# Second layer's second MLP product as seven half-size products, with sums of its rows made in the loop of the first product

## The chip, the cores and the metric

The kernel runs on one core of one Trainium2 chip. The metric is the device time of one execution in microseconds (us), as the median of several runs. The profile is that of one execution; times in it are counted from its first instruction.

## The reference

A two-layer encoder works on 1024 tokens of width 1024. Each layer adds three blocks to the residual stream x, each as `x = x + rms_norm(block(rms_norm(x)))`: a mixer (pooling and short convolution in the first layer, a state-space scan and a long convolution in the second), a cross attention to 256 memory rows, and an MLP. Everything is fp32. What the change touches is the MLP of the second layer:

```python
def squared_relu_mlp(xn, w1, w2):      # w1: 1024 x 4096, w2: 4096 x 1024
    h = jax.nn.relu(xn @ w1)
    return (h * h) @ w2

h = rms_norm(x, norm_mlp[i, 0])
x = x + rms_norm(squared_relu_mlp(h, mlp_w1[i], mlp_w2[i]), norm_mlp[i, 1])
```

## The kernel before, in words

Activations lie transposed, features on the 128 partitions and tokens along the row, in two halves of 512 tokens (`hf`). Every fp32 operand is split into a high part (fp32r, copied by ScalarE, L252) and a low remainder (subtracted by VectorE, L255 through L234), and every product is three matmuls, high by high, high by low and low by high (`mm3`, L259 to L263). A weight block of 128 x 1024 comes through `wblk` (L265): a DMA on SP's queue into one of two `raw` buffers, then the split into one of four `wp` buffers.

**First MLP product** (`mlp_up`, L675). It is already one step of Strassen's scheme over output features and tokens. The loop "ue" (L708, eight turns) makes the part that needs only the first operands, stores partial sums in DRAM (`P1`) and the first quarter of the hidden rows in DRAM (`HID`). The loop "up" (L728, sixteen turns) makes five more products per turn, of four k-blocks each, that is 5 x 4 x 3 = 60 matmuls of 512 columns. VectorE makes four weight sums (L734 to L737), two splits, a third split of half the size, and five additions of 128 x 512 (L751 to L761). ScalarE applies relu and square (L702). POOL's queue loads `P1` and stores the finished hidden rows, three DMAs a turn.

**Second MLP product** (`mlp`, L766). The hidden rows are cut in eight blocks `c` of 512. For each block, four weight blocks `np_` (256 output features each) meet both token halves: `down1` (L782) runs 2 x 4 x 3 = 24 matmuls of 512 columns into one PSUM tile, and VectorE adds the tile to an accumulator in SBUF (L794). Hidden rows come back from DRAM on POOL's queue two blocks of 128 x 1024 at a time (`load`, L772) and are split again. That is 8 x 4 x 2 x 24 = 1536 matmuls, of which the last 96 (block 7, second half) run as 192 matmuls of 256 columns (`last`, L803), so that the norm and the output of the first 256 tokens lie beside the matmuls of the others. `residual` (L380) ends a half: sum of squares, a norm factor made by TensorE and VectorE (`rms`, L307), scaling, addition of x, and the store.

**What sets the order.** The program is written as one sequence of generators; a scheduler places each engine's instructions ahead of time by the order of the program and by free buffers. Work under `high_priority` is placed before other work that is ready. Within an engine, and within a DMA queue, the order is then fixed: an instruction that waits holds all that is behind it. Buffers: `hp` 9 tiles of 8 KB a partition, `act` 8 of 8 KB, `wp` 4, `raw` 2, `tp` 3, `np` 3, PSUM 3 tiles of two banks (`mmp`) and 2 of one (`aux`).

Before the second MLP stands the cross attention (`attention`, L627): scores and softmax, then the output product (`proj_out`, L418) with its two residuals, whose loads and stores go over POOL's queue (L394, L400).

## Time and profile before

| | us |
|---|---|
| median of 3 runs | 2927.45 (2925.89 to 2929.41) |
| the profiled execution, its own time | 2933.49 |
| its span, first to last instruction | 2931.7 |
| TensorE busy / VectorE busy / ScalarE busy | 2804.3 / 1968.8 / 1046.2 |
| second layer, loop "ue" | from 2242 to 2335.5 |
| second layer, loop "up" | from 2335.5 to 2564 |
| second layer, second MLP product | from 2564 to 2914.5 |
| norm and output after the last product | from 2914.5 to 2931.7 |

How to read it: the three medians differ by 3.5 us, 0.12%. A busy time counts the time in which an engine had an instruction in work; for TensorE the instructions overlap, so that the distance between starts tells its rate, not the length of one. The stages above are cut where the first matmul of each starts in the trace.

### The profile page before, as it was taken

To read this page: it belongs to the slowest core of one execution; us is meant where nothing else is said; L and a number is where in the kernel's file an instruction comes from. 1 tells how busy PE (TensorE), PEld (TensorE's weight loads), DVE (VectorE), ACT (ScalarE), POOL (GpSimd) and SP (SyncE) were. 2 spreads that over 40 slices of the span, in tenths; PEclk is the share of its full clock that TensorE was granted. 3 is DMA by queue.
4 is the path that set the end of the run, shared out by engine and by line. 5 is a ranking of instruction groups with operands and counts; after the bars stand their busy time and mean duration, and the time that the engine had idled before them with its cause. 6 is when DMAs were issued, how large, how long until landed. Compare 5 with 4: busy or idle time off the path is not lost. (4 is left out here: it accounts for less than half of the span.)

```text
span 2931.7 us, 35820 instructions
## 1 busy us (share of the span) xinstructions
PE 2804.3 (96%) x14024; PEld 2343.6 (80%) x14024; DVE 1968.8 (67%) x3287; ACT 1046.2 (36%) x1260; POOL 219.8 (7%) x403
## 2 busy tenths in 40 slices
PE   7998999999999999999999898899999999999997
PEld 7877888988777877888788787678988788788886
DVE  6676546838898756794877777946738866534446
ACT  4353324434544441222342311243434544422210
POOL 0000000001211110010100000000001211100000
PEclk9999999999999999999999999999999999999999
DMA  5582214224644454342447778734226644433313
GB/s 176 212 280 101 69 51 136 96 86 164 225 173 151 151 189 131 115 160 68 155 152 236 258 240 283 251 122 137 87 72 209 233 150 149 160 119 101 103 56 115
DMA packets 159057, 448.81 MB, mean 153 GB/s; under 512 B 16356, under 2 KB 61544, under 8 KB 151848
## 3 DMA queue, kind: packets, MB, share of 16 engines
q1 hardware_dynamic: 79736, 219.81, 23.4%
q0 software_dynamic: 48496, 200.30, 19.7%
q10 hardware_dynamic: 30656, 26.41, 2.7%
q8 instruction: 110, 1.80, 0.3%
q14 instruction: 59, 0.48, 0.1%
HBM read 330.07 MB, written 116.39 MB: 152 GB/s over the span
## 5 line engine op out<-in xcount | busy, mean ns | idle before, releaser
L263 PE MATMUL mdn<-hdn,wdn 128*128 128x512 f32 x640 | 250.1, 391 | 0.0
L261 PE MATMUL mdn<-hdn,wdn 128*128 128x512 f32 x640 | 249.7, 390 | 0.0
L262 PE MATMUL mdn<-hdn,wdn 128*128 128x512 f32 x640 | 249.7, 390 | 0.0
L234 DVE TENSOR_TENSOR aup<-aup,mdn 128x1024 f32<-128x1024 f32 x108 | 131.5, 1218 | 169.8 <-PE mdn L263 169.6
L261 PE MATMUL mup<-apre,wup 128*128 128x512 f32 x384 | 151.9, 395 | 8.1 <-DVE hup L234 8.1
L234 DVE TENSOR_TENSOR hup<-hup,mup 128x512 f32<-128x512 f32 x128 | 87.5, 684 | 98.1 <-PE mup L263 96.9
L262 PE MATMUL mup<-apre,wup 128*128 128x512 f32 x384 | 150.3, 391 | 0.0
L263 PE MATMUL mup<-apre,wup 128*128 128x512 f32 x384 | 150.2, 392 | 0.0
L262 PEld LDWEIGHTS mdn<-hdn,wdn 128*128 128x128 f32 x640 | 120.3, 188 | 25.3 <-issue 0.6
L261 PEld LDWEIGHTS mdn<-hdn,wdn 128*128 128x128 f32 x640 | 120.4, 188 | 24.9 <-issue 0.2
L263 PEld LDWEIGHTS mdn<-hdn,wdn 128*128 128x128 f32 x640 | 120.3, 188 | 24.9
L252 ACT ACTIVATE wdn<-rdn 128x1024 fp32r<-128x1024 f32 x54 | 57.1, 1057 | 223.1 <-PE mdn L263 210.2
L252 ACT ACTIVATE wup<-rup 128x1024 fp32r<-128x1024 f32 x66 | 69.4, 1060 | 180.6 <-PE mup L263 165.7
L261 PE MATMUL msc<-wsc,hpre 128*128 128x256 f32 x448 | 127.9, 286 | 1.6 <-ACT hpre L252 1.6
L262 PE MATMUL msc<-wsc,hpre 128*128 128x256 f32 x448 | 128.9, 288 | 0.0
L263 PE MATMUL msc<-wsc,hpre 128*128 128x256 f32 x448 | 128.1, 287 | 0.4 <-DVE hpre L234 0.4
L262 PE MATMUL mmx<-hpre,wmx 128*128 128x512 f32 x320 | 124.7, 390 | 0.0
L261 PE MATMUL mmx<-hpre,wmx 128*128 128x512 f32 x320 | 124.7, 390 | 0.0
L263 PE MATMUL mmx<-hpre,wmx 128*128 128x512 f32 x320 | 124.5, 389 | 0.0
L234 DVE TENSOR_TENSOR wout<-rout,wout 128x1024 fp32r<-128x1024 f32 x48 | 58.6, 1222 | 87.3 <-ACT wout L252 87.3
L261 PE MATMUL mue<-hpre,wue 128*128 128x512 f32 x256 | 101.1, 395 | 2.2 <-ACT tue L252 2.2
L261 PE MATMUL mout<-asc,wout 128*128 128x512 f32 x256 | 100.0, 391 | 0.0
(503 smaller groups left out, 7902.7 us busy)
## 6 DMA issues: line engine op xcount, KB each, us to landing
hup<-mlp_w SPq DMA_DIRECT2D x32, 1024.0 KB, 5.3
rdn<-mlp_w SPq DMA_DIRECT2D x62, 512.0 KB, 3.7
tdn<-HID POOLq DMA_DIRECT2D x48, 512.0 KB, 3.9
nres<-x POOLq DMA_DIRECT2D x44, 512.0 KB, 4.9
x<-hout POOLq DMA_DIRECT2D x32, 512.0 KB, 5.2
rue<-mlp_w SPq DMA_DIRECT2D x32, 512.0 KB, 3.9
HID<-hup POOLq DMA_DIRECT2D x32, 512.0 KB, 2.9
wmx<-fwd POOLq DMA_DIRECT2D x16, 1024.0 KB, 7.3
```

The lines of the kernel that those rows point to most:

```text
L234: self.nc.vector.tensor_tensor(out=out, in0=a, in1=b, op=op)
L252: self.nc.scalar.activation(out, a, AF.Copy)
L261: t.matmul(out, l[0], r[0], start=start, stop=False, **kw)
L262: t.matmul(out, l[0], r[1], start=False, stop=False, **kw)
L263: t.matmul(out, l[1], r[0], start=False, stop=stop, **kw)
```

## The change

The product of hidden rows (4096 x 1024 tokens) and weights (4096 x 1024 features) of the second layer is cut in two by two quarters of the hidden rows and tokens, and of the features, and made as seven products of half the size in each direction (16 k-blocks, 4 feature blocks, 512 tokens, three matmuls). Each of the seven is 28 / 7 = 4 steps of two 128-row pairs, 48 matmuls a step.

- The hidden operands of the seven (`HO`) are made in the loop "up" of the first product: two stored as they are, one copied from the end of the relu, four made by VectorE in a new tile `e` (four subtractions of 128 x 512) and stored by one DMA. A load of the first quarter (`e[:, 0]`) is added. The weight sums of the turn `p + 1` are now written ahead of the products of the turn `p` (`prep`), in both layers; in both, the 1 MB weight load becomes two of 512 KB, and in the second layer other buffers and another order of the same four sums are used.
- The weight operands: four are blocks or a stored sum (one load each), three are differences of two loaded blocks, subtracted by VectorE at the load. The sum `S1` is made in DRAM during the attention by eight copies and eight accumulating DMAs on POOL's queue (`down_sums`). `S2` is stored on ScalarE's queue where the third product makes it, and read by the seventh.
- Products 1, 3 and 5 start new PSUM tiles; 2, 4, 6 and 7 go on adding in the tiles of the one before. After each product VectorE or ScalarE takes the two tiles out once; there is no accumulator that is read and written per block any more.
- The last two steps of the seventh product run as 256-column matmuls in two token groups, as `last` did.

```diff
-        for p in range(16):
+        def prep(p):
             with self.tc.high_priority():
...
+                    pools = [self.np_ if j % 5 in (0, 2, 4) else self.raw for j in range(3 * p, 3 * p + 3)]
...
+        nxt = prep(0)
+        for p in range(16):
+            c, S1, S2, S3, S4, A22 = nxt
+            if p < 15:
+                nxt = prep(p + 1)
+            if HO is not None:
+                to = HO[:, p // 2, :, (p % 2) * 512:(p % 2 + 1) * 512].rearrange("i p t -> p i t")
+                with self.tc.high_priority():
+                    e = self.hslot([4, 512])
+                    nc.gpsimd.dma_start(e[:, 0], to[:, 0])
...
+                nc.gpsimd.dma_start(HID[p, 0, :, 512:1024] if HO is None else to[:, 1], c[:, 1])
+            if HO is not None:
+                nc.gpsimd.dma_start(to[:, 6], c[:, 3])
+                self.sub(e[:, 1], c[:, 2], e[:, 0])
+                self.sub(e[:, 3], c[:, 3], c[:, 2])
+                self.sub(e[:, 2], c[:, 3], e[:, 1])
+                self.sub(e[:, 0], c[:, 1], e[:, 2])
+                nc.gpsimd.dma_start(to[:, 2:6], e[:])
...
+    def down_sums(self, l, after):
...
+        nc.gpsimd.dma_start(S1[:, 0, 0:1].rearrange("n c -> c n"), after.bitcast(F32)[0:1, 0:8])
+        for n in range(9):
+            if n < 8:
+                nc.gpsimd.dma_start(S1[n], w2[n, 1, 0])
+            if n > 0:
+                nc.gpsimd.dma_start(S1[n - 1], w2[n - 1, 1, 1], accum_op=ALU.add, max_dma_last_dim=4096)
+
+    def mlp_q(self, l, B, xsrc, xdst, gnext, res):
...
+        prods = [(True, (a11,), 0), (False, (a12,), 1), (True, (s1, a11), 4), (False, (a11, a21), 5),
+                 (False, (a22,), 2), (True, (s1,), 3), (False, (a12, s2), 6)]
+        steps = [(i, c) for i in range(7) for c in range(0, 8, 2)]
+
+        def hload(i, c):
+            t = self.tmp([2, 512])
+            nc.gpsimd.dma_start(t[:].rearrange("p a t -> p (a t)"), HO[prods[i][2], c])
+            h = self.hslot([2, 2, 512], F32R)
+            self.split(h[:, 0], h[:, 1], t[:])
+            return h
+
+        def wload(i, c):
+            src = prods[i][1]
+            if len(src) == 1:
+                return self.wblk(src[0](c))
+            r = self.slot([2, 1024])
+            for k in range(2):
+                nc.sync.dma_start(r[:, k], src[k](c))
+            self.sub(r[:, 0], r[:, 0], r[:, 1])
+            w = self.wp.tile([P, 2, 1024], F32R, tag="w", name=self.nm("w"))
+            self.split(w[:, 0], w[:, 1], r[:, 0])
+            if i == 2:
+                nc.scalar.dma_start(S2[c], r[:, 0])
+            return w
...
+        for j, (i, c) in enumerate(steps):
+            if i == 6 and c == 4 and gnext is None:
+                break
+            (ws, hs), nxt = nxt, load(j + 1) if j + 1 < len(steps) else None
...
+            for t in range(2):
+                run(t, ws, hs, i, c == 0 and prods[i][0], c == 6)
+                if c == 6:
...
+                        elif i == 2:
+                            self.add(c12[:, at], U[:, at], ps[t][:])
...
+        self.down_sums(1, H[1][7][0])
         H = self.attention(1, self.GV[1], H, x1, x2)
...
-        merge((self.mlp(1, H, x2, self.out, None, []), 1))
+        merge((self.mlp_q(1, H, x2, self.out, None, []), 1))
```

The first layer keeps `mlp`.

## Rows read from the trace of the kernel before

**Rows 1.** The page's first part: the span, and busy time of each engine.

```profile
span 2931.7 us, 35820 instructions
...
PE 2804.3 (96%) x14024; PEld 2343.6 (80%) x14024; DVE 1968.8 (67%) x3287; ACT 1046.2 (36%) x1260; POOL 219.8 (7%) x403
```

**Rows 2.** Busy time by stretch: early loads, first layer's "up", then second layer's stages.

```profile
core 0: us, PE busy (x) PEld busy (x) DVE busy (x) ACT busy (x) POOL busy (x), PEclk, DMA share, GB/s
150.00:190.00 40.00, 39.63 (x165) 24.20 (x164) 33.77 (x53) 23.95 (x26) 3.20 (x6) 1.00 1.01 363
808.00:1040.00 232.00, 226.30 (x996) 180.69 (x995) 196.17 (x538) 102.52 (x121) 30.53 (x55) 1.00 0.48 165
2242.00:2335.50 93.50, 92.10 (x406) 73.84 (x405) 79.27 (x104) 54.02 (x55) 21.98 (x41) 1.00 0.68 226
2335.50:2564.00 228.50, 225.69 (x971) 181.50 (x970) 145.89 (x193) 105.04 (x121) 28.57 (x53) 0.99 0.47 160
2564.00:2890.00 326.00, 325.95 (x1441) 269.49 (x1440) 142.25 (x137) 69.16 (x68) 17.49 (x33) 1.00 0.30 97
2890.00:2914.50 24.50, 24.27 (x200) 23.80 (x198) 15.75 (x37) 4.42 (x7) 0.53 (x1) 1.00 0.38 126
```

**Rows 3.** Two matmuls of the second product, a hundred starts apart (timeline of TensorE).

```profile
2669.21 0.39 PE L261 MATMUL mdn<-hdn,wdn 128*128 128x512 f32 x1
...
2691.87 0.39 PE L262 MATMUL mdn<-hdn,wdn 128*128 128x512 f32 x1
```

**Rows 4.** Groups by line in the second product: busy us, mean ns, idle before and releaser.

```profile
L234 DVE TENSOR_TENSOR aup<-aup,mdn 128x1024 f32<-128x1024 f32 x52 | 63.4, 1219 | 120.8 <-PE mdn L263 120.8
...
L234 DVE TENSOR_TENSOR hdn<-tdn,hdn 128x1024 fp32r<-128x1024 f32 x24 | 29.3, 1223 | 36.4 <-ACT hdn L252 36.4
L234 DVE TENSOR_TENSOR wdn<-rdn,wdn 128x1024 fp32r<-128x1024 f32 x24 | 29.3, 1219 | 16.7 <-ACT wdn L252 16.7
...
L252 ACT ACTIVATE wdn<-rdn 128x1024 fp32r<-128x1024 f32 x24 | 25.4, 1058 | 142.2 <-PE mdn L263 142.2
```

**Rows 5.** DMA issues of the page: KB each, median us from issue to landing.

```profile
rdn<-mlp_w SPq DMA_DIRECT2D x62, 512.0 KB, 3.7
...
rue<-mlp_w SPq DMA_DIRECT2D x32, 512.0 KB, 3.9
HID<-hup POOLq DMA_DIRECT2D x32, 512.0 KB, 2.9
...
VW<-n ACTq DMA_DIRECT2D x8, 512.0 KB, 9.2
```

**Rows 6.** Groups by line in second layer's "up": an addition of half the size.

```profile
L234 DVE TENSOR_TENSOR hup<-hup,mup 128x512 f32<-128x512 f32 x63 | 43.2, 685 | 66.7 <-PE mup L263 66.2
```

**Rows 7.** One turn of second layer's "up" (timeline): VectorE twice, then ScalarE's last square.

```profile
2426.67 1.41 DVE L234 TENSOR_TENSOR hup<-hup,mup 128x512 f32<-128x512 f32 x2 [3.92 <-PE mup L263]
...
2440.51 1.41 DVE L234 TENSOR_TENSOR hup<-hup,mup 128x512 f32<-128x512 f32 x2 [3.89 <-PE mup L263]
...
2436.71 0.63 ACT L704 ACTIVATE hup<-hup 128x512 f32<-128x512 f32 x1
```

**Rows 8.** TensorE's waits (us, times, longest): second layer's "up", then first layer's "up".

```profile
PE mup L261 <- DVE hup L234: 2.4, 2, 2.0
...
PE mup L261 <- DVE hup L234: 5.7, 5, 1.7
```

**Rows 9.** Second attention (timeline): its last input tile, POOL's gap, "ue"'s operand and start.

```profile
2101.58 1.08 ACT L252 ACTIVATE hpre<-npre 128x1024 fp32r<-128x1024 f32 x1
...
2067.59 0.53 POOL L400 DMA_DIRECT2D x<-hout  x1 [4.20 <-DVE hout L234]
2198.93 0.54 POOL L394 DMA_DIRECT2D nres<-x  x1 [130.80 <-DVE nout L234]
...
2235.76 1.22 DVE L234 TENSOR_TENSOR hpre<-npre,hpre 128x1024 fp32r<-128x1024 f32 x1
...
2241.99 0.39 PE L261 MATMUL mue<-hpre,wue 128*128 128x512 f32 x1
```

More of the change, by code (lines that the diff above doesn't have):

```diff
@@ L132, in prep @@
     w2 = a["mlp_w2"].reshape(2, 8, 4, P, 4, 256)
-    o["mlp_w2"] = np.transpose(w2, (0, 1, 4, 3, 2, 5)).reshape(2, 8, 4, P, 1024)
+    o["mlp_w2"] = np.transpose(w2, (0, 1, 4, 3, 2, 5)).reshape(2, 8, 4, P, 1024)[:1]
+    w2 = a["mlp_w2"][1:].reshape(1, 8, 2, 2, P, 2, 512)
+    o["mlp_w2q"] = np.transpose(w2, (0, 1, 5, 3, 4, 2, 6)).reshape(1, 8, 2, 2, P, 1024)
     o["pool_w"] = np.transpose(a["ev_pool_w"][0], (1, 0, 2)).reshape(P, 512)
@@ L200, in __init__ @@
         self.GV = {}
+        self.S1 = {}
         self.consts()
@@ L723, in mlp_up @@
                 square(t[:], ps[:])
-                for i in range(2):
-                    nc.gpsimd.dma_start(HID[p + i, 0, :, 0:512], t[:, i])
+                if HO is not None:
+                    nc.gpsimd.dma_start(HO[0, p // 2], t[:].rearrange("p a t -> p (a t)"))
+                else:
+                    for i in range(2):
+                        nc.gpsimd.dma_start(HID[p + i, 0, :, 0:512], t[:, i])
             yield
         self.lab = f"up{l}"
-        for p in range(16):
+        def prep(p):
@@ L729, in mlp_up @@
             with self.tc.high_priority():
-                r = self.hslot([2, 1024])
-                nc.sync.dma_start(r[:], w1[2 * p:2 * p + 2].rearrange("n p c -> p n c"))
-                x, y = [self.raw.tile([P, 2, 512], F32, tag="r", name=self.nm("r")) for _ in range(2)]
-                a11, a12, a21, a22 = r[:, 0, :512], r[:, 0, 512:], r[:, 1, :512], r[:, 1, 512:]
-                self.add(y[:, 1], a21, a22)
-                self.sub(x[:, 0], y[:, 1], a11)
-                self.sub(y[:, 0], a11, a21)
@@ L737, in mlp_up @@
-                self.sub(x[:, 1], a12, x[:, 0])
-                S2, S4 = parts(x[:].rearrange("p a b -> p (a b)"))
-                S3, S1 = parts(y[:].rearrange("p a b -> p (a b)"))
+                if HO is None:
+                    h = self.hslot([2, 1024])
+                    r = [h[:, i] for i in range(2)]
+                    x, y = [self.raw.tile([P, 2, 512], F32, tag="r", name=self.nm("r")) for _ in range(2)]
+                else:
+                    pools = [self.np_ if j % 5 in (0, 2, 4) else self.raw for j in range(3 * p, 3 * p + 3)]
+                    r = [t.tile([P, 1024], F32, tag="n" if t is self.np_ else "r", name=self.nm("r"))[:] for t in pools]
+                    y = r.pop().rearrange("p (a t) -> p a t", a=2)
@@ new lines, in prep @@
+                for i in range(2):
+                    nc.sync.dma_start(r[i], w1[2 * p + i])
+                a11, a12, a21, a22 = [t[:, i:i + 512] for t in r for i in (0, 512)]
+                if HO is None:
+                    self.add(y[:, 1], a21, a22)
+                    self.sub(x[:, 0], y[:, 1], a11)
+                    self.sub(y[:, 0], a11, a21)
+                    self.sub(x[:, 1], a12, x[:, 0])
+                    S2, S4 = parts(x[:].rearrange("p a b -> p (a b)"))
+                    S3, S1 = parts(y[:].rearrange("p a b -> p (a b)"))
+                else:
+                    self.add(y[:, 1], a21, a22)
+                    self.sub(y[:, 0], y[:, 1], a11)
+                    self.sub(a11, a11, a21)
+                    self.sub(a12, a12, y[:, 0])
+                    S2, S1 = parts(y.rearrange("p a b -> p (a b)"))
+                    S3, S4 = parts(r[0])
@@ L740, in mlp_up @@
                 w = self.tmp([2, 512], F32R)
                 self.split(w[:, 0], w[:, 1], a22)
-                A22 = (w[:, 0], w[:, 1])
                 c = self.hslot([4, 512])
                 nc.gpsimd.dma_start(c[:, 0], P1[p])
+            return c, S1, S2, S3, S4, (w[:, 0], w[:, 1])
+        nxt = prep(0)
[8 more added lines that the diff above has]
+                    nc.gpsimd.dma_start(e[:, 0], to[:, 0])
@@ L757, in mlp_up @@
                 square(c[:, 2:4], c[:, 2:4])
[L758 removed]
+                if HO is None:
+                    nc.gpsimd.dma_start(HID[p, 1].rearrange("p (a t) -> p a t", a=2), c[:, 2:4])
             prod(cd[:, 0], A22, B["T4"], True)
@@ L762, in mlp_up @@
                 square(c[:, 1], c[:, 1])
-                nc.gpsimd.dma_start(HID[p, 0, :, 512:1024], c[:, 1])
+                nc.gpsimd.dma_start(HID[p, 0, :, 512:1024] if HO is None else to[:, 1], c[:, 1])
+            if HO is not None:
+                nc.gpsimd.dma_start(to[:, 6], c[:, 3])
[4 more added lines that the diff above has]
+                nc.gpsimd.dma_start(to[:, 2:6], e[:])
             yield
@@ L859, in mlp @@
                 res.append(finish(hf, acc))
+    def down_sums(self, l, after):
+        nc = self.nc
+        w2 = self.i["mlp_w2q"][l - 1]
+        self.S1[l] = S1 = self.dram([8, P, 1024], f"SA{l}")
+        nc.gpsimd.dma_start(S1[:, 0, 0:1].rearrange("n c -> c n"), after.bitcast(F32)[0:1, 0:8])
[4 more added lines that the diff above has]
+                nc.gpsimd.dma_start(S1[n - 1], w2[n - 1, 1, 1], accum_op=ALU.add, max_dma_last_dim=4096)
```

92 lines of the change are left out of this document (90 added, 2 removed).

## The prediction

> **What bounds the kernel now.** I read the page's busy times first: TensorE has work in hand for 2804.3 of 2931.7 us, VectorE for 67% [rows 1]. That is an average, so the next view is busy time by stretch [rows 2]. In the second layer's second product TensorE is busy for 325.95 of 326 us and then 24.27 of 24.5, while VectorE is at 142.25 of 326 (44%) and the DMA engines at 0.30. A busy TensorE may still be slow, so the third view is its timeline: a hundred starts of 512-column matmuls take 2691.87 - 2669.21 = 22.66 us, 0.2266 each, at a granted clock of 1.00, which is the 2.4 GHz level [rows 2, 3]. The 1440 of them (1536 less the 96 that run as 192 halves) make 1440 x 0.2266 = 326.3 us: the whole stage. So here nothing but the number of matmuls sets the time, and a matmul less is 0.2266 us less, as long as its operands come in time.
>
> The profiled execution took 2933.49 us, 1.8 more than its span; the median of the runs is 2927.45. I sum against the profiled one and move the result down by the 6.0 us between them. A difference under 0.2% (5.9 us) counts as none.
>
> **Matmuls removed.** Seven products of 4 steps of 48 matmuls are 1344 in place of 1536. The last two steps run as 192 of 256 columns, as before, so 1440 - 1248 = 192 of 512 columns go: 192 x 0.2266 = **-43.5 us**. All of it lies on the path, by [rows 2].
>
> **The new second product, engine by engine.** A step is 48 x 0.2266 = 10.9 us of TensorE. VectorE and ScalarE each split two hidden and two weight tiles in it, VectorE at 1.22 us, ScalarE at 1.06 [rows 4]; in the 12 steps of the third, fourth and seventh product VectorE also makes two differences of the same size. That is 4.9 or 7.3 us of VectorE, 4.2 of ScalarE, in 10.9. In the last step of a product two evictions of 1.22 us come on top: 9.8 at most. In return the 64 accumulations into SBUF (52 of them under one name in [rows 4]) become four times two, and the last ones. "ue" ran with VectorE at 79.27 of 93.5 us, TensorE at 92.10 [rows 2]: a share of 85% hides. So I cost VectorE and ScalarE at nothing; if that cover goes, two-block steps pay the excess over 10.9 us each. Where a product goes on in the tiles of the one before, TensorE waits for the copy of the first tile; 24 matmuls (5.4 us) on the second tile cover that 1.2 us.
>
> **Its DMAs.** A tile is 512 KB, 0.524 MB. A one-block step moves four (2.10 MB in 10.9 us, 193 GB/s), a two-block step six (289), and a step of the third product eight, since two stores of `S2` are added (385). "ue" moved 226 GB/s over 93.5 us at a share of 0.68, which is 226 / 0.68 = 332 at a full share; the highest stretch moved 363 at a share of 1.01 over 40 us, with TensorE still busy for 39.63 [rows 2]. The third product's 16.8 MB take 16.8 / 0.363 = 46.2 us at the one rate and 16.8 / 0.332 = 50.5 at the other, against 43.5. So it gives back 2.7 to 7.0 us, or nothing if buffers let its loads start in the second product, which needs only 193. I take **+2.7**, since the row with the full share shows what the engines reach. The Trainium skill (DMA: Bandwidth & Descriptors, Specifications) gives a limit of about 358 GB/s of HBM for a core; by that rule the stage would take 46.9 us and the term would be +3.4; the 363 of the stretch stands just above it. The other two-block products need 12.6 / 0.332 = 37.9 us and fit.
>
> **Queues.** SP issues 80 weight loads here in place of 32, POOL 56 hidden loads in place of 32, ScalarE 8 stores. POOL is busy 17.49 of 326 us now [rows 2], and so has room. A store of `S2` waits for VectorE's difference, but the ScalarE split behind it reads the same one: nothing more is held. Two `raw` buffers serve one-block steps: landing 3.7 to 3.9 us [rows 5] and a split of 1.06 + 1.22 make 6.2 us a pair of loads against 10.9. Cost nothing.
>
> **The loop "up" of the second layer.** Added per turn: four subtractions of 0.685 us [rows 6], a load of `e`, and a store more (POOL: five issues a turn in place of three, each 28.57 / 53 = 0.54 each [rows 2], 2.7 of a turn's 13.84). VectorE has an idle stretch of 3.9 us in each turn of 13.84, before the first addition of the next [rows 7]. The last subtraction needs the last square, which ScalarE ends at 2437.34, 3.2 us before that stretch does; the other three can run ahead of it. So 2.7 us fit into 3.9, but VectorE goes from 145.89 to 145.89 + 64 x 0.685 = 189.7 of 228.5 us, 83%. The first layer's "up" ran at 196.17 of 232, 85%, with other work beside it, and TensorE waited 5.7 us for VectorE there against 2.4 here [rows 2, 8]. Bounds: the waits may vanish, since sums are prepared a turn ahead (-2.4), or become the first layer's (+3.3). I take **+3.3**, the row that is nearest in load. Behind the store of `e`, which waits for the last subtraction, POOL's queue holds the next `e` and `P1` loads; both are wanted most of a turn later. Traffic grows by the 1 MB store and is about 3.1 MB a turn, 228 GB/s: "ue" bore that.
>
> The first layer's turns are only written in another order, with two loads for one on SP: its waits of 5.7 us bound a gain, and as much a loss. I take 0, as the weight sums were already made a turn ahead by priority. One store for two in "ue": nothing.
>
> **The sum made in DRAM.** It starts when the attention's input is ready, at 2101.58 + 1.08 [rows 9]. POOL then waits for each copy, and a copy stands behind the accumulation issued before it, so it is held for some 8 x (copy + accumulation). No row has either kind. Bounds from stores of that size are 2.9 and 9.2 us [rows 5]: 8 x 5.8 = 46 us to 8 x (2.9 + 9.2) = 97. POOL's next work in the old order comes at 2198.93, 96 us later, and the first operand of "ue" was ready 5.0 us before TensorE took it (2241.99 - 2236.98) [rows 9]. Both ends are covered: **0**. The same 5.0 us is what a longer hold uses up first.
>
> **The end.** The last weight blocks can be split only when the step before gives back `wp` buffers: 2 x (1.06 + 1.22) = 4.6 us at most, against 24 matmuls of 24.27 / 200 = 0.12 us, 2.9 us, that run first [rows 2, 4]. Bounds 0 and 4.6 - 2.9 = 1.7; I take **+1.0**. The norm and output after it are unchanged.
>
> Sum: -43.5 + 2.7 + 3.3 + 1.0 = **-36.5**. 2933.5 - 36.5 = 2897.0 profiled, and **2891** as a median.
>
> **The rivals.**
>
> 1. *The transfers do not reach their rate.* The new product mixes loads, stores and DRAM-side reads on three queues. At 290 GB/s the third product takes 57.9 us instead of 46.2 and the fourth and seventh just fit (43.4): 11.7 us more, **2903**. For it: the 289 and 385 GB/s stand above the 226 that a whole stage has shown. Against it: [rows 2], the first stretch. Chance 0.20.
> 2. *The accumulations hold POOL.* If one takes 14 us, the hold is 8 x 16.9 = 135 us, 39 longer than the gap; less the 5 us of slack, "ue" starts 34 us late and the gain is gone: **2925**. It decides from 9.5 us on. Nothing in the trace shows an accumulation; for it is only that it reads twice per write. Chance 0.07.
> 3. *Slower: the two `raw` buffers.* If a load lands later than 10.9 - 2.3 = 8.6 us, the 16 one-block steps last as long as landing and split. At 10.9 us of landing 16 x 2.3 eats the whole gain; at 12 us it is 16 x 3.4 = 54 us: **2945**. For it: 9.2 us of landing occurs [rows 5]. Against it: 3.9 in "ue", at a higher load than one-block steps have. Chance 0.06.
> 4. *More than forecast.* No stall in the third product, no waits in either "up": -43.5 - 2.4 - 2 = -48, **2880**. Chance 0.05.
>
> That the matmuls are not saved is no rival: the loops fix 1344. The forecast keeps 0.62.
>
> **The numbers.** The forecast's own terms run from -43.5 - 2.4 to -43.5 + 7.0 + 3.3 + 1.7, so 2881 to 2896. The range is 2880 to 2912: it takes in rival 1 and some room for waits that add, and leaves out rivals 2 and 3. Faster by over 0.2%: 0.62 + 0.20 + 0.05, and a part of rival 2, 0.02: 0.89. Slower: rival 3 with the far end of 2, 0.07. The same: 0.04.
>
> **What would show it.** Right: 192 fewer 512-column matmuls; TensorE in the new product busy for all but some 5 us; the third product's stretch 44 to 51 us at a DMA share near 1, the others 43 to 44; "up" 229 to 233 us; `nres` of the attention issued at about 2199 as before. Wrong: waits of TensorE on weight or hidden tiles in steps of one block, VectorE waiting for DMAs there, an "up" turn over 14.1 us, or "ue" starting after 2242.

## The result and the profile after

The changed kernel takes 2912.61 us (2911.12 to 2913.44), the kernel before 2928.43 in the same comparison: a ratio of 0.9945 (95% interval 0.9931 to 0.9959). That is faster by about 16 us, less than half of the 36.5 forecast, and just above the forecast's range of 2880 to 2912. The profiled execution took 2913.07 us, 20.4 less than the one of before.

The page's first part answers to [rows 1].

```profile
span 2911.3 us, 35912 instructions
...
PE 2767.3 (95%) x13832; PEld 2311.9 (79%) x13832; DVE 2038.3 (70%) x3375; ACT 1088.0 (37%) x1304; POOL 260.3 (9%) x468
```

14024 - 13832 = 192 matmuls are gone, as the change says. TensorE's busy time fell by 37 us, but the span by only 20.4, so waits came. To find them I set the first matmul of each stage in TensorE's timeline against the same one of before (us; the last column is the best kernel of the experiments):

| stretch | before | after | best |
|---|---|---|---|
| start to first layer's "up" | 805.9 | 806.2 | 806.1 |
| first "up" to second mixer | 622.2 | 626.6 | 618.7 |
| second mixer | 612.0 | 609.8 | 609.7 |
| second attention's scores | 110.1 | 114.8 | 107.5 |
| its output projection | 91.8 | 91.9 | 91.8 |
| second "ue" to last matmul | 672.4 | 645.1 | 627.9 |
| end | 17.3 | 16.9 | 17.2 |

(The best kernel's first stretch holds a first mixer 6.5 us longer and an opening 6.3 us shorter; the opening varied by itself, from 207 to 216 us, over the runs.) Of the 43.5 us that the matmuls are worth, 27.3 arrive in the second layer's MLP. Another 4.4 and 4.7 are lost in two places ahead of it. Busy time by stretch (columns as in [rows 2]), for the first "up", then the second layer's "ue", "up", the new product and the end:

```profile
806.20:1044.30 238.10, 227.49 (x986) 181.08 (x985) 193.84 (x528) 101.98 (x120) 30.54 (x55) 0.99 0.45 156
2249.30:2335.80 86.50, 86.33 (x381) 69.35 (x380) 76.09 (x100) 52.86 (x54) 15.60 (x30) 1.00 0.66 219
2335.80:2563.10 227.30, 223.16 (x962) 179.85 (x962) 177.53 (x249) 99.23 (x115) 48.08 (x84) 0.99 0.65 225
2563.10:2894.40 331.30, 320.00 (x1481) 265.65 (x1479) 198.44 (x213) 123.20 (x126) 34.18 (x64) 0.98 0.69 245
2894.40:2911.30 16.90, 1.87 (x9) 1.27 (x7) 11.45 (x33) 0.63 (x1) 0.00 (x0) 0.61 0.30 103
```

These parts are not cut quite like those of [rows 2]: there 2564 is where the last "up" turn ends, while the first matmuls of the second product, mixed with that turn, start at 2552.3; here 2563.1 is the first such matmul, and the last "up" turn ends at 2576.6. So the two kernels are compared from "ue" to the last matmul. In [rows 2] TensorE was busy in the second product for all but 0.05 us of 326; here it is idle for 11.3 of 331.3, some of which are the last "up" turn's. TensorE's waits in the second MLP (us in total, times, longest), to set beside [rows 8]:

```profile
PE mdn L265 <- ACT wdn L256: 7.5, 1, 7.5
PE mup L265 <- DVE hup L238: 7.0, 5, 2.9
PE mdn L265 <- DVE adn L238: 0.3, 1, 0.3
```

So there is one long wait on a weight split, in the third product, and 4.6 us more of waits in "up". The waits of the first layer's "up", the last group of [rows 8], have grown too, from 5.7 to 8.2 + 1.7 + 0.5:

```profile
PE mup L265 <- DVE hup L238: 8.2, 6, 2.5
PE xup L265 <- ACT wup L256: 1.7, 1, 1.7
...
PE xup L267 <- DVE wup L238: 0.5, 1, 0.5
```

**The third product.** Four windows around its wait, then SP's waits in it (its next loads are `L951`), then VectorE's timeline:

```profile
2650.00:2660.00 10.00, 10.00 (x46) 8.28 (x45) 3.84 (x4) 4.91 (x5) 0.70 (x2) 1.00 1.03 415
2660.00:2670.00 10.00, 10.00 (x46) 8.29 (x45) 6.11 (x7) 3.98 (x4) 1.06 (x2) 1.00 0.85 277
2670.00:2680.00 10.00, 6.91 (x31) 5.39 (x29) 4.96 (x5) 2.12 (x2) 1.06 (x2) 0.98 1.02 388
2680.00:2690.00 10.00, 5.51 (x13) 3.88 (x13) 7.94 (x7) 3.90 (x4) 0.53 (x1) 0.51 0.82 289
```

```profile
SPq L951 <- DVE wdn L238: 16.6, 3, 14.3
SPq L951 <- DMA SB<-adn: 16.0, 2, 12.4
```

```profile
2659.00 1.23 DVE L238 TENSOR_TENSOR hdn<-tdn,hdn 128x1024 fp32r<-128x1024 f32 x1 [5.79 <-ACT hdn L256]
2660.14 1.22 DVE L238 TENSOR_TENSOR adn<-adn 128x1024 f32<-128x1024 f32 x1
...
2677.03 1.23 DVE L238 TENSOR_TENSOR adn<-adn 128x1024 f32<-128x1024 f32 x1 [2.06 <-DMA adn<-mlp_w2q]
2679.74 1.23 DVE L238 TENSOR_TENSOR adn<-adn 128x1024 f32<-128x1024 f32 x1 [1.49 <-DMA adn<-mlp_w2q]
...
2684.43 4.63 DVE L238 TENSOR_TENSOR wdn<-adn,wdn 128x1024 fp32r<-128x1024 f32 x4 [1.12 <-ACT wdn L256]
```

Read from below: TensorE waits until 2684.45 for splits; in front of them on VectorE stand differences (`adn<-adn`) that wait for loads; the loads were late because SP stood for up to 14.3 us at a buffer; and the buffers were held because a difference of landed blocks ran only at 2660.14, behind a split at which VectorE had idled for 5.79 us. The windows show the other half: 415 GB/s for 10 us, then 277 while SP stood. After the wait the granted clock is 0.51, the 1.2 GHz level: the next twelve matmuls, from 2684.45 to 2690.00, take 5.55 us where twelve at 0.2266 take 2.72, so 2.8 us more.

**The second attention.** Loads of `G` and the sum's transfers there, from issues by kind (KB each, median us to landing), after and then before, then the window and TensorE's wait in it, and the same wait before:

```profile
SA<-mlp_w2q POOLq DMA_DIRECT2D x16, 512.0 KB, 8.5
rsc<-G SPq DMA_DIRECT2D x2, 512.0 KB, 9.1
```

```profile
rsc<-G SPq DMA_DIRECT2D x2, 512.0 KB, 3.1
```

```profile
2120.00:2140.00 20.00, 16.42 (x125) 15.89 (x124) 9.01 (x19) 8.16 (x22) 4.76 (x7) 0.92 1.04 303
```

```profile
PE xsc L626 <- DVE tsc L621: 3.7, 3, 3.4
```

```profile
PE xsc L622 <- DVE tsc L617: 0.5, 3, 0.2
```

The DMA engines are full (1.04), a weight load lands after 9.1 us in place of 3.1, and TensorE idles for 3.6 of 20 us.

### The profile page after: what moved, and what is told of

Its sections match the earlier page's. It is cut to its first block, busy times and chain, and to the rows that moved or that the text cites. A ratio compares the mean times of both kernels' runs of the same rounds, so it can differ in the third digit from the quotient of the medians.

```text
span 2911.3 us, 35912 instructions
## 1 busy us (share of the span) xinstructions
PE 2767.3 (95%) x13832; PEld 2311.9 (79%) x13832; DVE 2038.3 (70%) x3375; ACT 1088.0 (37%) x1304; POOL 260.3 (9%) x468
## 5 line engine op out<-in xcount | busy, mean ns | idle before, releaser
L265 PE MATMUL mdn<-hdn,wdn 128*128 128x512 f32 (+1 forms) x752 | 287.4, 382 | 7.8 <-ACT wdn L256 7.5
L266 PE MATMUL mdn<-hdn,wdn 128*128 128x512 f32 (+1 forms) x752 | 287.4, 382 | 0.0
L267 PE MATMUL mdn<-hdn,wdn 128*128 128x512 f32 (+1 forms) x752 | 287.2, 382 | 0.0
L265 PEld LDWEIGHTS mdn<-hdn,wdn 128*128 128x128 f32 x752 | 142.0, 189 | 36.3 <-ACT wdn L256 8.3
L266 PEld LDWEIGHTS mdn<-hdn,wdn 128*128 128x128 f32 x752 | 142.0, 189 | 27.5 <-issue 0.6
L267 PEld LDWEIGHTS mdn<-hdn,wdn 128*128 128x128 f32 x752 | 142.0, 189 | 27.4 <-DVE wdn L238 1.0
L238 DVE TENSOR_TENSOR hdn<-tdn,hdn 128x1024 fp32r<-128x1024 f32 x74 | 90.4, 1222 | 52.3 <-ACT hdn L256 52.0
L256 ACT ACTIVATE hdn<-tdn 128x1024 fp32r<-128x1024 f32 x74 | 78.2, 1056 | 124.6 <-PE mdn L267 100.3
```

Of the source, the lines that this page charges most:

```text
L238: self.nc.vector.tensor_tensor(out=out, in0=a, in1=b, op=op)
L256: self.nc.scalar.activation(out, a, AF.Copy)
L265: t.matmul(out, l[0], r[0], start=start, stop=False, **kw)
L266: t.matmul(out, l[0], r[1], start=False, stop=False, **kw)
L267: t.matmul(out, l[1], r[0], start=False, stop=stop, **kw)
```

## The experiments

The theory was that the matmuls' 43.5 us were real and four separate losses gave a part back: the third product, the DRAM sum, and both layers' "up" loops. Times by stage are read as in the table above. The kernel before took from 2914.55 to 2938.3 us over all these comparisons, so a stage is the better witness for a few microseconds. The edits are shown shortened; where a line is in words or has a remark behind `#`, it stands for several lines of code.

**First layer in its old order.**

```
-                for i in range(2):
-                    nc.sync.dma_start(r[i], w1[2 * p + i])
+                if HO is None:      # first layer; the second as changed
+                    nc.sync.dma_start(h[:], w1[2 * p:2 * p + 2].rearrange("n p c -> p n c"))
...
+            if HO is None and p > 0:
+                nxt = prep(p)
...
-            if p < 15:
+            if HO is not None and p < 15:
                 nxt = prep(p + 1)
```

> Only the first layer's "up" loop goes back to the order of the kernel before: its weight pair comes in one transfer of 1 MB, and the turn's preparation stands in its own turn, not one turn ahead. The second layer stays as changed. Theory (four separate losses, one of them the first layer's reordered turns): from the start of the first layer's "up" to the start of the second mixer the time falls from 626.6 us back to the 622.3 of before, TensorE's waits in that loop fall from some 13.9 us in sum to some 6, and the whole from 2912.6 to about 2908.5 (2906 to 2911). Rival (those 4.3 us come from where buffers and transfers happen to stand, not from the order): within 1 us of the changed kernel's 626.6, and the whole within 1.5 us of 2912.6.

From "up" to the second mixer: 621.6 us, 5.0 less than 626.6. TensorE's waits in the loop:

```profile
PE mup L265 <- DVE hup L238: 5.8, 5, 1.8
```

That is the row of before again. The whole: 2900.84 (2898.31 to 2908.9), ratio 0.9923 (0.9896 to 0.9951). In the nine experiments that take the old turns back the stretch takes 615.2 to 621.6 us; in the changed kernel and the nine experiments that keep the new ones, 622.4 to 630.2. So the rewritten turns cost this, which I had costed at 0 within 5.7 either way. Two things went back together, the order and the one load in place of two; no run parts them in the first layer. In the second layer, below, the order alone was changed.

**The sum in DRAM moved to the first mixer.**

```
-        self.down_sums(1, H[1][7][0])        # ahead of the second attention
+                if j == 0: self.down_sums(1, y[:, 0])   # first mixer
```

> The sums in DRAM (eight copies, eight accumulating transfers) are issued in the first mixer, behind the first of its convolution outputs, where POOL issues nothing between 276 and 710 us and the DMA share is 0.08 to 0.37, instead of ahead of the second attention. Theory (they collide with the attention's weight loads): the second attention's scores fall from 114.8 us to the 110.1 of before, the load that took 9.07 us lands in 3 to 4 again, and the first layer's MLP still starts at 711.8 (0.7 either way): the whole about 2908 (2906 to 2910). Rival (the same traffic hits the mixer's weight loads in its turn): the scores gain 4.7 and the first MLP starts 3 us or more later; the whole within 2 us of 2912.6. Second rival (the 4.7 us are not the sums' doing): scores within 1 us of 114.8.

The scores took 106.3 us instead of 114.8, and the first MLP began at 710.3. The mixer takes 300.2 us with the transfers and 300.1 without them: there they do no harm. Over all the experiments the scores take 113.8 to 117.3 us with the sum ahead of them, and 106.2 to 107.9 with it elsewhere. 106.3 is even 3.8 less than before: a wait of 2.5 us for the norm at the stage's start is gone too, since the order of the work there moved; I did not follow that. The whole: 2905.12 (2891.13 to 2910.46), ratio 0.9924 (0.9893 to 0.9955).

**The third product: is it the store, its buffer, or its queue?** First without the store (the last product takes S1 where it took S2), then with the difference in a tile of its own, then with the store on GpSimd's queue.

```
-            if i == 2: nc.scalar.dma_start(S2[c], r[:, 0])
```

> The third product's difference is not stored, and the last product takes the stored sum S1 where it took S2, so that its loads stay as many (the lower right part of the output is computed from other weights). Theory (the third product waits because its load buffers are held until their stores have landed): TensorE's wait of 7.5 us in the third product and the eight matmuls at half clock behind it go, 8 to 9 us, the whole about 2904 (2902 to 2906). Rival A (the 16.8 MB alone are more than the product's 43.5 us take): 4.2 MB less, so the same 8 to 9 us; the next kernel tells these apart. Rival B (VectorE stands behind the splits of the hidden tiles, and the store has no part in it): the wait stays over 4 us, the whole above 2909.

```
+            f = self.ntmp([1024])[:] if i == 2 else r[:, 0]
-            self.sub(r[:, 0], r[:, 0], r[:, 1])      # split and store r[:, 0]
+            self.sub(f, r[:, 0], r[:, 1])            # split and store f
```

> The third product's difference is written to a tile of the normalisation's pool (three buffers, idle at this place), split and stored from there; the load buffer is free as soon as VectorE has read it. Bytes, transfers and operations are as many as in the changed kernel. Theory (buffers held by the stores): the 7.5 us wait falls below 2 us, the whole to 2904 to 2907. Rival A (bytes alone): the wait stays over 5 us, the whole within 2 us of 2912.6. Rival B (VectorE's order behind the hidden tiles' splits): the same as rival A's numbers; a kernel with that order changed follows.

```
-                nc.scalar.dma_start(S2[c], r[:, 0])
+                nc.gpsimd.dma_start(S2[c], r[:, 0])
```

> The changed kernel with the third product's store issued from GpSimd's queue instead of ScalarE's; nothing else. Theory (the store is issued late because ScalarE's queue stands at a weight split that waits for a buffer of TensorE's, and the load behind it on SP waits until that store has landed): the wait of 7.5 us falls by 3 us or more, to the 4.6 that stayed without any store. Rival (the place of the store's issue is of no consequence): the wait stays at 6.5 us or more, the whole within 1.5 us of 2912.6. Second rival (the hidden tiles' loads, on the same queue, now stand behind the store's wait): a wait on a hidden tile.

TensorE's waits in the down stage, one fence for each in that order:

```profile
PE mdn L265 <- ACT wdn L256: 4.6, 1, 4.6
```

```profile
PE mdn L265 <- ACT wdn L256: 4.7, 1, 4.7
PE mdn L267 <- DVE wdn L238: 3.6, 2, 3.3
```

```profile
PE mdn L265 <- ACT wdn L256: 7.5, 1, 7.5
```

With 4.2 MB less and no store at all 4.6 us stay (2906.11 us, ratio 0.9938, 0.9919 to 0.9958); with the buffer freed early 8.3 in three waits, two of them long (2914.10, 0.9962, 0.9948 to 0.9975); the queue is of no account (2914.12, 0.9967, 0.995 to 0.9985). Where a kernel leaves this product as it is, the wait is 7.5 to 8.9 us (five kernels) and the down stage 330.0 to 333.7. My first theory, buffers held by stores, explains 3 to 4 us at most. It fell.

**Is it the hidden tiles' splits, or too few buffers?**

```
             self.split(h[:, 0], h[:, 1], t[:])
+            # third and fourth product: tensor_copy and subtract on nc.gpsimd
```

> For the third and fourth products the hidden tiles are split on GpSimd, both halves; loads, stores, bytes and the weights' work on VectorE and ScalarE stay. Theory now (the run without the store and the run with another tile kept waits of 4.6 to 8 us, so neither the store nor the buffer explains most of it; VectorE stands 5.8 us idle behind a hidden tile's split, whose buffer TensorE still reads, while landed weight pairs wait in line for their difference): without those splits in line the differences run as their loads land, and the third product's wait falls below 2 us, the down stage from 331.3 to about 323 to 325. Rival A (the bytes: 16.8 MB in 43.5 us): the wait stays over 5 us. Rival B (GpSimd is too slow for the splits): a wait on a GpSimd line of line 943 or 944 in place of the one on the weights.

```
-            r = self.slot([2, 1024])
+            r = slot([2, 1024]) if c is even, else two tiles of the np and raw pools
```

> The changed kernel with the paired loads of every second chunk going to two tiles of the pools that the up loop used for them, so that some seven pairs can be under way or waiting instead of five; bytes, stores and operations are the same. Theory (a load can't be issued while earlier pairs stand in too few buffers behind VectorE's and ScalarE's order, and transfers that stand for 11 to 13 us aren't made up, since the product needs nearly all of the rate): the third product's wait falls from 7.5 to under 3 us, the down stage from 331.3 to about 324 to 327. Rival (bytes alone, 16.8 MB in 43.5 us): the wait stays at 6 us or more, the down stage within 2 us of 331.3.

Without the hidden splits in line the wait is no shorter (2911.01 us, ratio 0.995, 0.993 to 0.9969):

```profile
PE mdn L265 <- ACT wdn L256: 8.3, 1, 8.3
```

VectorE's differences then stood behind a weight split that waited for a buffer of TensorE's; one thing at the head of the line had taken the place of another. TensorE had no wait on a split of GpSimd's. But the run is not clean: beside GpSimd's work seven of VectorE's differences took 2.1 us on average, up to 3.4, in place of 1.23 (the last part of these experiments shows why), so it does not rule out the hidden splits. More buffers moved the wait about: 5.0 us stayed in the third product, 4.6 came in the fourth and 4.3 in the last, where half the pairs now take a `raw` buffer, the pool of the single loads ahead of them (2927.03 us, ratio 0.9992, 0.9981 to 1.0004). Neither theory brought its gain.

**Is it the bytes?** Two runs on top of the best kernel (below), whose third product loads one block, with an idle load and store a chunk.

```
+            if i == 2:  # nc.gpsimd in the first run, nc.sync in the second
+                dma_start(self.ntmp([1024])[:], a11(c)); dma_start(X[c], U[:, 0:2])
```

> The fastest run so far, whose third product loads one block a chunk, with 512 KB loaded to a tile that nothing reads and 512 KB stored from a finished tile for each of its chunks, from GpSimd's queue: the 16.8 MB of the changed kernel's third product, without its difference, without paired buffers and without a wait of a store on a result. Theory (the third product waits by buffers and order: loads stand while earlier pairs wait in line on VectorE and ScalarE, and what stands isn't made up): no wait of TensorE over 1.5 us in the third product, the down stage within 2 us of that run's 315.9. Rival (bytes: 16.8 MB need more than the product's 43.5 us): a wait of 3 us or more in the third product or at the fourth's start, the down stage 319 or more.

> As the run with the third product's bytes but without its difference, with the idle load and the idle store issued from SP's queue, each behind its chunk's block, so that they fall into the product's own time (from GpSimd's queue they had all landed by 2628.6 us, ahead of the product). Theory (order and buffers, not bytes): no wait of TensorE over 1.5 us in the third product, the down stage within 3 us of the 315.9 of the fastest run. Rival (bytes in the product's own time): a wait of 3 us or more, the down stage 319 or more.

Neither had a wait in the third product; the down stage took 321.7 us, with a wait of 4.1 in the last "up" turn, and 317.7 (2897.39 us, ratio 0.9901, 0.988 to 0.9922; and 2901.07, 0.9899, 0.9877 to 0.992). But both times the idle transfers ran ahead, into the second product and before; so these two don't settle it. The next one does, with everything in place but the differences (the third and seventh products multiply other weights):

```
-            self.sub(r[:, 0], r[:, 0], r[:, 1])
+            if i != 2: self.sub(r[:, 0], r[:, 0], r[:, 1])
```

> The changed kernel with the third product's eight differences left out: both blocks of a pair are loaded to the same buffers, the first is split and stored as it is (the third and seventh products multiply other weights). Bytes, buffers, loads and stores are as many, and fall into the product's own time. Theory (the differences' place in VectorE's order holds the buffers and with them the load queue): the 7.5 us wait falls under 3 us, the down stage from 331.3 to 322 to 326. Rival A (bytes in the product's own time): a wait of 6 us or more. Rival B (the buffers, which are held until the store has landed): 4 us or more with SP waiting for the stores.

Busy time in the four windows as above:

```profile
2650.00:2660.00 10.00, 10.00 (x46) 8.29 (x45) 3.85 (x5) 5.53 (x6) 0.53 (x1) 1.00 1.03 411
2660.00:2670.00 10.00, 10.00 (x46) 8.29 (x45) 3.85 (x4) 4.47 (x5) 1.06 (x2) 1.00 0.95 330
2670.00:2680.00 10.00, 10.00 (x46) 8.28 (x45) 5.50 (x5) 3.14 (x4) 1.06 (x2) 1.00 1.01 407
2680.00:2690.00 10.00, 10.00 (x45) 8.27 (x45) 5.77 (x5) 3.36 (x4) 1.06 (x2) 1.00 0.74 278
```

TensorE is busy for all of it. Bytes, buffers and stores are those of the changed kernel, whose transfers in 44 us come first, this run's second:

```profile
DMA packets 4211, 15.33 MB, mean 348 GB/s; under 512 B 473, under 2 KB 473, under 8 KB 4208
```

```profile
DMA packets 4469, 16.33 MB, mean 371 GB/s; under 512 B 490, under 2 KB 490, under 8 KB 4466
```

The down stage takes 320.7 us, 10.6 less, near the 7.5 + 2.8 read above; the whole 2905.21 (2899.14 to 2910.65), ratio 0.9922 (0.9897 to 0.9948). SP still waits in it, for up to 9.8 us at a time:

```profile
SPq L951 <- DMA SB<-adn: 12.5, 4, 8.5
SPq L951 <- DMA adn<-mlp_w2q: 9.8, 1, 9.8
```

So it is the differences that make TensorE wait, and neither the bytes, since 16.3 MB fit into 44 us, nor a waiting SP by itself. That they act through VectorE's order is read from its timeline; no run parts the order from the eight operations' own time. VectorE was busy for 3.8 to 7.9 us of each 10, so it was not short of time.

**The second layer's "up".** First without its four subtractions and the load for them (the third to sixth products multiply other rows):

```
-                self.sub(e[:, 1], c[:, 2], e[:, 0])     # and three more
-                nc.gpsimd.dma_start(to[:, 2:6], e[:])
+                nc.gpsimd.dma_start(to[:, 2:6], c[:])
```

> The second layer's "up" loop leaves out its four row subtractions and the load that they need; the rows that it has are stored in their place, so that the stores stay as large (the third to sixth products multiply other rows than they should). Theory (the four subtractions of about 0.69 us a turn on VectorE cost the loop some 4 us of TensorE's waits): the stage from the loop's start to the first down matmul falls from 227.2 us to about 223 (222 to 224.5), and the waits in it, 3.5 us at the end included, fall under 3 us. Rival (VectorE has room for them, and the loop's waits are its weight preparation's as in the kernel before): the stage stays within 1 us of 227.2.

```profile
PE mup L265 <- DVE hup L238: 7.0, 5, 2.6
```

The same 7.0 us; the stage 227.9 for 227.2 (2910.69 us, ratio 0.9948, 0.9932 to 0.9963). The subtractions cost nothing that shows: the term of +3.3 had a wrong cause.

**Both weight sums made once, in the first mixer.** VectorE makes `S1` and `S2` chunk by chunk there, and the third product loads `S2` as one block. The second run adds the first layer's old order.

```
-        prods: (True, (s1, a11), 4)      + S2 stored in the third product
+        prods: (True, (s2,), 4)
+        x = a21 + a22 -> S1; z = x - a11 -> S2    # self.add, self.sub, a chunk a mixer step
```

> Both weight sums (a21+a22 and a21+a22-a11) are made once, in the first mixer, by VectorE from three loads a chunk, and stored from there; no copy or accumulating transfer is made ahead of the second attention. The third product then loads one block a chunk as the first two do, without a difference and without a store; the fourth and seventh still load two. Theory (the third product's wait is a matter of its paired loads with the difference): no wait of TensorE over 1 us in the third product, and the stage from the first down matmul to the last, 331.3 us, falls by 8 to 9.5 us to some 322.5; the second attention's scores fall from 114.8 to about 107 to 110; the first mixer gains not more than 2 us. The whole 2897 to 2901. Rival (pairs only need to come next somewhere: the wait moves to the fourth product, where the next paired loads stand): a wait of 3 us or more there, the down stage not below 327. Second rival (the mixer's VectorE is held by the new loads): the first attention starts 3 us or more later than 513.8.

> The run with both weight sums made by VectorE in the first mixer, and the first layer's "up" loop in the order of the kernel before. If the four losses are separate, their gains add up: 4.9 us in the first layer's MLP, 5 to 8 in the second attention's scores, 8 to 9 in the third product, from 2912.6 to about 2893 (2889 to 2897), a ratio to the kernel before of 0.988 to 0.990. Rival (the gains are given back where the next wait ends last): not below 2900.

The down stage falls from 331.3 to 320.8 us with no wait, and the scores to 107.3, but the first mixer takes 320.9 us instead of 300.1 (324.2 in the second run): 2917.28 us, ratio 0.9962 (0.9946 to 0.9978), and 2909.54, 0.9942 (0.9927 to 0.9958). The second rival of the first was right. In the mixer, TensorE's wait, and VectorE's for the sums' loads:

```profile
PE mmx L265 <- ACT amx L256: 18.1, 1, 18.1
```

```profile
DVE nmx L238 <- DMA nmx<-mlp_w2q: 44.5, 12, 8.9
```

It is the pattern of the third product again, in a place where I had put it myself. So, with the first layer's old order kept, the sums go to GpSimd; and the run after that also prepares the second layer's "up" in its own turn.

```
-                self.add(x[:], x[:], y[:]); self.sub(z[:], x[:], z[:])
+                nc.gpsimd.tensor_tensor(...)          # both
```

> As the run with the mixer's sums and the old order in the first layer, but both sums of a chunk are made by GpSimd, which has nothing else between 276 and 710 us, so that no engine of the mixer stands behind a load of theirs. Theory (the mixer lost its 21 to 24 us because VectorE stood in order at a sum whose loads took up to 8 us, ahead of the mixer's weight splits): the first attention starts at 514 (1.5 either way) instead of 534.7, the other gains stay (first MLP's up loop to second mixer some 617 to 622 us, second attention's scores 106 to 107.5, down stage 320.8), the whole about 2888 (2885 to 2892), a ratio to the kernel before of 0.986 to 0.988. Rival (it is the 33.6 MB of traffic of the sums that delays the mixer's weights, whichever engine adds): the first attention starts at 520 or later.

```
-            if HO is not None and p < 15: nxt = prep(p + 1)
+            if p > 0: nxt = prep(p)                    # both layers
```

> The run before with one more edit: the second layer's "up" loop too prepares a turn's weights in its own turn instead of one turn ahead. Theory (in both layers the preparation one turn ahead puts a difference, whose load has not landed, ahead of the adds that free TensorE's buffers: VectorE stood 3.99 us at one before the wait of 2.19 us in the second turn): the waits in the loop fall from some 7 us to 3, the time from the start of "ue" to the last matmul by 3 to 5 us against the run before, the whole to about 2884. Rival (with five buffers for raw pairs and sums, the own-turn order leaves too little time for the loads): the waits grow, the whole is 2 us or more above the run before. Second rival (the loop's waits are the subtractions' and the stores', not the order's): within 1.5 us of the run before.

The first: 2894.14 us (2890.83 to 2898.18), ratio 0.9877 (0.9858 to 0.9895), 6 above what was expected, as the mixer still takes 308.3. Its rival had forecast that: the attention starts at 524.3, and "520 or later" was the sign for the traffic. The last run below parts traffic from arithmetic. (The 33.6 MB in it is a slip: 24 loads and 16 stores of 512 KB are 21 MB.) The second: **2884.67 us** (2880.95 to 2892.93), ratio **0.985** (0.9831 to 0.987), the best kernel here and ahead of both. From "ue" to the last matmul it takes 4.1 us less than the first. Without the idle transfers, the four kernels of that order take 627.9 to 630.5 us there, and the four with the preparation one turn ahead and no wait in the third product 632.0 to 635.6. TensorE's waits in "up", the first run's and then the second's, and the second's busy time from "ue" on:

```profile
PE mup L265 <- DVE hup L238: 6.8, 6, 3.0
```

```profile
PE mup L265 <- DVE hup L238: 3.2, 3, 2.1
```

```profile
2233.80:2545.70 311.90, 308.10 (x1341) 247.89 (x1341) 253.56 (x348) 152.32 (x168) 64.59 (x114) 1.00 0.67 226
2545.70:2861.70 316.00, 315.29 (x1481) 263.20 (x1480) 188.46 (x204) 122.87 (x126) 33.31 (x63) 1.00 0.66 229
```

The wait of 2.1 us in the second turn stays in either order; what went is the others, and the half-clock matmuls behind them.

**The mixer's remaining 6.5 us.** Three runs on the best kernel: sums begun later, sums by transfers alone with a negation on ScalarE, and the traffic without GpSimd's arithmetic (the third, sixth and seventh products multiply other weights).

```
+                nc.gpsimd.tensor_copy(t[0][:, 0:8], after)   # begins beside the output projection
```

> The fastest run so far (both sums made by GpSimd, both up loops prepared in their own turn) with the sums begun later: a first small copy on GpSimd reads the last convolution output, so that the sums run beside the first mixer's output projection, where VectorE has little to do. Theory (GpSimd's sums stretch VectorE's operations, from 1.22 to some 3 us where both work, and that cost the mixer 6.5 to 8.3 us): the mixer falls from 306.6 to 308.3 us to 300 to 301.5, the rest stays, the whole to about 2878 (2875 to 2883). Rival (the sums' three tiles are then missing to the residual of the projection's first half, which stands behind them): the first attention starts no earlier, 306 us or more after the mixer's start, the whole 2884 or more.

```
+                accumulate S1 += a22; copy S2 <- S1; accumulate S2 += -a11   # ScalarE: scale=-1.0
```

> The fastest run so far with both sums made by transfers in the first mixer: copy of a21, accumulating transfer of a22, copy of the sum, accumulating transfer of the negative of a11, which ScalarE makes (eight operations of about 1 us); GpSimd computes nothing. Theory (the mixer's loss of 6.5 to 8.3 us came of GpSimd's sums stretching VectorE's operations from 1.22 to some 3 us): the mixer takes 300 to 301.5 us instead of 306.6, the rest stays, the whole to about 2877 (2874 to 2881), a ratio to the kernel before of 0.982 to 0.985. Rival (traffic or ScalarE's wait for a load hold the mixer's weights): 303 us or more.

```
-                nc.gpsimd.tensor_tensor(...)          # both
```

> The fastest run so far without GpSimd's two operations a chunk in the mixer: all loads and stores stay, the stored blocks are a21 and a11 in place of the sums (the third, sixth and seventh products multiply other weights than they should). Theory (GpSimd's arithmetic stretches VectorE's operations, and the mixer's 6.5 us are that): the mixer takes 300 to 301.5 us, VectorE's weight splits there 1.2 us a piece again instead of 1.75. Rival (traffic: the mixer's loads land later beside the sums' 20 MB): 304 us or more with the splits at 1.2 us.

The first is slower than the kernel before, 2955.81 us, ratio 1.0108 (1.0086 to 1.013): the rival came, and the mixer takes 377.6 us. The sums hold the three tiles that the residual needs, and TensorE stands behind it:

```profile
PE mout L265 <- ACT nout L349: 71.3, 1, 71.3
```

The second takes 2898.80, ratio 0.9885 (0.9867 to 0.9902): ScalarE waits for the loads as VectorE did, and the mixer takes 316.8.

```profile
ACT nmx L925 <- DMA nmx<-mlp_w2q: 31.2, 7, 9.7
```

The third settles it: with the traffic alone the mixer takes 299.8 us (the whole 2882.11, ratio 0.9857, 0.9785 to 0.9929; two timed runs are too few to set that against the best kernel's). VectorE's weight splits between 240 and 400 us, in the best kernel and then here:

```profile
L238 DVE TENSOR_TENSOR wmx<-rmx,wmx 128x1024 fp32r<-128x1024 f32 (+1 forms) x13 | 22.8, 1753 | 36.1 <-ACT wmx L256 36.0
```

```profile
L238 DVE TENSOR_TENSOR wmx<-rmx,wmx 128x1024 fp32r<-128x1024 f32 (+1 forms) x13 | 15.4, 1182 | 43.7 <-ACT wmx L256 43.6
```

1753 ns against 1182 for the same splits: GpSimd's sums stretch VectorE's operations. A place that costs nothing was not found for both sums; for S1 alone, made by transfers, the mixer was one (300.2 us, above).

## Why the prediction was wrong

The mechanism and its size were right: 192 matmuls are gone, each worth 0.2266 us on the path, and the best kernel's 627.9 us from "ue" to the last matmul are 44.5 less than before. What was wrong are the costs, by the forecast's own steps:

- **Third product's DMAs, +2.7.** It cost 7.5 us of waiting and 2.8 in slow matmuls behind it, 10.3 in all. The step asked only whether the bytes fit, and they do: 16.33 MB in 44 us without a wait. What failed is the sentence on VectorE and ScalarE costed at nothing. It added up their busy time (7.3 of 10.9 us), but not the order: a difference stands in line with splits that wait for TensorE's buffers, and the next load waits for the difference. That the differences do it is shown; which operation they stand behind was read, and varied only for the hidden tiles, in a run that is not clean. On the rate: the Trainium skill (HBM Reference, Specifications) has about 425 GB/s for a core that streams alone, beside the 358 for a share of two; the window of 415 agrees with the first. The 363 that the step took for what the engines reach was passed too, by 371 over 44 us.
- **The sum in DRAM, 0.** It cost 4.7 us in the scores. The step looked at who waits for POOL, and that part was right. It did not ask whose loads share the DMA engines while 16 transfers run: two weight loads of the attention that landed at 9.1 us in place of 3.1. The copies and accumulations landed after 8.5 us in the median, within the bounds of 2.9 to 9.2, and the last was issued at 2143 us, long before POOL's next work at 2206, so rival 2 did not happen. Of the forecast's signs of being wrong, "ue" after 2242 came, at 2249.3, by this loss and the first layer's.
- **First layer's turns, 0.** They cost 4.4 us, inside the bound of 5.7. "Already made a turn ahead by priority" was the wrong reading; going back to the old turns gives the 5 us back.
- **Second layer's "up", +3.3.** The waits grew by 4.6 us, near enough, but by another cause. Without the subtractions they stay; without the preparation one turn ahead they fall to 3.2. Luck, then, as to the number.
- **The end, +1.0.** 16.9 us for 17.3, and no wait over 0.3 us in the last steps of the product.
- **Rivals.** The first (transfers do not reach their rate) came nearest in time, 2903, but not in cause: they reach 415 GB/s when they are issued. The third, slower: one-block steps show no wait. The fourth's time needs all the losses gone, and the best kernel comes within 5 us of it.

Sum of the second MLP: -43.5 + 7.5 + 2.8 + 4.6, and 1.8 more than before for half-clock matmuls after the waits in "up", less 1.2 for small waits elsewhere, is -28.0; measured -27.3.

## What to carry to other kernels

Adding up an engine's busy time against the step it hides under is not enough: for each added operation, ask what stands ahead of it in its engine's order, what that waits for, and which load waits for the buffer it frees. Work that is prepared earlier also stands earlier in its engine's order; where it waits there for a load, all that is behind it waits too. Bulk transfers that "nobody waits for" still set the landing time of those that somebody does, so put them where the stretch has neither a full DMA share nor loads on the path.

## What the runs showed of the hardware

GpSimd's arithmetic is not free for VectorE. While GpSimd added blocks of 128x1024, VectorE's subtractions of that size took up to 3.1 us in the best kernel's mixer, where they take 1.22 alone, and the mixer 306.6 us instead of 299.8. The Trainium skill (SBUF — State Buffer, Who interferes with whom) says that a VectorE operation with two inputs in SBUF contends with GpSimd's reads; the two runs above agree, 1753 ns against 1182.

A wait of TensorE can cost more than it lasts. Behind the one of 7.5 us the clock was at 0.51, and twelve matmuls took 2.8 us more than at 0.2266 each; behind one of 2.2 us in "up" eight came 0.39 to 0.43 us apart, 1.8 us more in all:

```profile
2354.00:2358.00 4.00, 3.21 (x9) 2.53 (x10) 4.00 (x7) 0.09 (x1) 0.00 (x0) 0.66 0.00 0
```

But not every such wait is followed by the lower clock. Behind waits in "up" of 2.1 us (best kernel), 2.4 (without the store) and 2.9 (hidden splits on GpSimd) the matmuls went on at 0.22 to 0.24 us from the second on. What decides it is not shown here.
